# A third buffer for x projections, a group norm whose second part is written two projections later, and three 1/rms chains instead of five

## The chip, the cores and the metric

The kernel runs on one core of one Trainium2 chip. Its time is the device time in microseconds of one execution. Three executions of the kernel before took 2889.99 us in the median (2886.86 to 2891.28). The change is judged by the same time of the changed kernel.

## The reference

One inference step of a decoder trunk with two layers, on 16 meta tokens plus 1024 prompt tokens and on 8 sampled sequences of 8 tokens (1104 rows of 1024 features). Layer 0 is a Mamba-2 mixer and a SwiGLU feed-forward; layer 1 is sliding-window attention and a SwiGLU feed-forward. The change touches the mixer alone:

```
u   = rmsnorm(h) ; z, xBC, dt = split(u @ w_in)        # 1/rms of each row
x,B,C = silu(conv4(xBC) + b)                            # causal conv of width 4
y   = SSD(x * dt, a, B, C) + D * x                      # chunks of 128, 4 groups
v   = y * silu(z)
v   = v * rsqrt(mean over a group's 512 features of v*v + eps) * gain
h   = h + v @ w_out
```

Each of the four groups has 512 x features (four tiles of 128), 128 B and 128 C features, 512 z features and its own norm.

## The kernel before, in words

Each fp32 matrix product is done as three matmuls on split operands (L73 to L75: high by high, high by low, low by high). Features lie on partitions and rows (tokens) on the free dimension. The mixer goes over the rows in two halves: the first has 592 columns (80 sampled and meta rows, then 512 prompt rows; five blocks), the second 512 (four blocks). A projection is one 128-wide column tile of `w_in` against all rows of the half: 48 matmuls of 296 columns in the first half, 24 of 512 in the second. Its weights are loaded, split by ScalarE (L150) and by VectorE or GpSimd (L156), and kept in DRAM for the second half.

In each half four groups follow one another. Beside the SSD of group g (`ssd`, `chunk_in`, `chunk_out`, and in the first half `decode`, which carries the eight sampled states through TensorE) the function `fill_pieces` writes the dense work, one projection at a time: four z projections with the gate of group g-1 (`gate`), the norm of group g-1, the projections of group g+1 (`xbc`: B, C, then four x tiles, each followed by its conv on ScalarE and VectorE), and the output projection of older groups (`out`, which adds into the residual, L832). Beside the last group, g = 3, there is no g+1, and z of group 3 is projected ahead into a tile of the x tag (`gate_ahead`).

`norm` is a generator in two parts. The first sums the squares by a matmul with ones (L803), scales (L804) and computes 1/rms by ten small VectorE instructions (`rsqrt`, L89 to L98). The second spreads the factors over partitions: for each block VectorE makes a diagonal matrix (L811), TensorE multiplies it with ones into an accumulator of the projections' own ring (L812; two accumulators in the first half, three in the second); then VectorE scales each x tile (L816), ScalarE and VectorE split it (L79, L80) into yH and yL for `out`. The tag xT, which holds the four x tiles of a group or z of group 3, has two buffers, so that x of group g+1 reuses the buffer of group g-1, which is free when the norm of g-1 has read it.

The order on each engine is written by a planner that works with its own model of the durations, with the order of the program as priority; the SSD is written with a priority 300 ahead of the dense work. Each engine then goes through its queue in that fixed order.

At the start `input_half` goes over the blocks: square with a row sum on ScalarE (L370), scale (L372), the `rsqrt` chain, transposes of the raw rows (L382), the scaled rows (L387), their transposes (L392) and the split. In the second half blocks go in pairs through one chain, in the first each block has its own. At the end of the mixer `out` of the last group in the second half saves each finished residual tile to DRAM (`FeedForward.save`, L1261), with the DMA issued from SP.

Of the kernel before, what the change touches and what calls it, by code (L numbers as in the profile page):

```python
# [10 lines left out]
F32 = mybir.dt.float32  # L11
# [66 lines left out]
def split_copy(nc, H, L, src):  # L78
    nc.scalar.copy(H, src)  # L79
    nc.vector.tensor_tensor(L, src, H.bitcast(F32), ALU.subtract)  # L80
# [130 lines left out]
def load_params(K, I):  # L211

    nc = K.nc
    buf = K.scratch
    row = 0
    for nm, n in GAINS:
        src = I["ffn_norm_g"][int(nm[3])] if nm.startswith("ffn") else (I[nm] if nm in ("kv_norm_g", "final_norm_g") else I[nm][0])
        nc.sync.dma_start(buf[row : row + n, 3072:3200], src.rearrange("(k p) -> k p", p=128))
        row += n
    for i, nm in enumerate(("ssm_dt_bias", "ssm_A_log", "ssm_D")):  # L220
        nc.sync.dma_start(buf[:, 3200 + 32 * i : 3232 + 32 * i], I[nm][0].partition_broadcast(128))
    nc.sync.dma_start(buf[:4, :3072], I["ssm_conv_w"][0])
    nc.sync.dma_start(buf[4:5, :3072], I["ssm_conv_b"])
    nc.sync.dma_start(buf[32:56, :3072], I["state_conv"][0].rearrange("b k c -> (b k) c"))
# [44 lines left out]
class Mamba:  # L269
# [59 lines left out]
    def input_half(self, hf):  # L329
        nc, K = self.nc, self.K  # L330
        self.u = []
        for nm in ("uH", "uL"):
            for i in range(2):
                self.u.append(self.up.tile([128, 4, 592], F32R, name=f"{nm}{i}", tag=f"{nm}{i}"))
        H2, L2 = self.u[:2], self.u[2:]
        self.uH = [H2[k // 4][:, k % 4, :] for k in range(KD)]
        self.uL = [L2[k // 4][:, k % 4, :] for k in range(KD)]
        blocks = HALVES[hf]["blocks"]
        rows = {}

        def load(c):
            if c < len(blocks):
                rows[c] = self.load_rows(hf, c)

        if hf == 0:
            v = self.small([128, 2], "xv")
            nc.gpsimd.memset(v[:], 0.0)
            nc.scalar.activation(v[:, 0:1], v[:, 1:2], AF.Square)
        for c in range(2):
            load(c)  # L350
        gb = [self.tmp("gb") for _ in range(2)]
        for i in range(2):
            nc.sync.dma_start(gb[i][:, :512], self.I["ssm_norm_g"][0, 512 * i : 512 * i + 512].partition_broadcast(128))
        if hf == 0:
            for c in range(2, 5):
                load(c)
            load_params(K, self.I)
            self.wdt = self.kp.tile([128, KD, 32], F32, name="wdt")
            nc.sync.dma_start(self.wdt[:], self.I["ssm_w_in"][0, :, 5120:5152].rearrange("(k p) m -> p k m", p=128))
        self.rtok = []  # L360
        groups = ((0,), (1,), (2,), (3,), (4,)) if hf == 0 else ((0, 1), (2, 3))
        for cs in groups:
            nr = blocks[cs[0]][1]
            v = self.small([128, 2], "xv")
            xns = [self.quad("xn") for _ in cs]
            if hf == 1 and cs[0] == 0:
                for c in range(2, 4):
                    load(c)
            for i, c in enumerate(cs):
                nc.scalar.activation(xns[i][:nr], rows[c][:nr], AF.Square, accum_out=v[:nr, i : i + 1])  # L370
            w = v[:nr, : len(cs)]
            nc.vector.tensor_scalar(w, w, 1.0 / D, EPS, ALU.mult, ALU.add)  # L372
            r = rsqrt(nc, self.wk, w, len(cs), f"rx{cs[0]}")
            self.rtok += [r[:, i : i + 1] for i in range(len(cs))]
            for i, c in enumerate(cs):
                o, n = blocks[c]
                xr, xn = rows[c], xns[i]
                for kh in range(2):
                    ps = self.ps()
                    for j in range(4):  # L380
                        k = 4 * kh + j
                        nc.tensor.transpose(ps[:, 128 * j : 128 * j + n], xr[:n, 128 * k : 128 * k + 128], K.ident[:n, :n])  # L382
                    eng = nc.scalar.copy if kh else nc.vector.tensor_copy
                    eng(K.h[hf][:, 4 * kh : 4 * kh + 4, o : o + n], ps[:].rearrange("p (k c) -> p k c", k=4)[:, :, :n])
                for kh in range(2):
                    ks = slice(512 * kh, 512 * kh + 512)
                    nc.vector.scalar_tensor_tensor(xn[:n, ks], xr[:n, ks], r[:n, i : i + 1], gb[kh][:n, :512], ALU.mult, ALU.mult)  # L387
                for kh in range(2):
                    ps = self.ps()
                    for j in range(4):  # L390
                        k = 4 * kh + j
                        nc.tensor.transpose(ps[:, 128 * j : 128 * j + n], xn[:n, 128 * k : 128 * k + 128], K.ident[:n, :n])  # L392
                    pv = ps[:].rearrange("p (k c) -> p k c", k=4)[:, :, :n]
                    split_copy(nc, H2[kh][:, :, o : o + n], L2[kh][:, :, o : o + n], pv)
                yield
            if hf == 0 and 1 in cs:
                self.W.load()
# [140 lines left out]
    def xbc(self, hf, g, which):  # L538
        G = self.Gs[g]
        if 0 in which:  # L540
            G.BC = [None] * 2
        for i in which:
            wH, wL = self.W.get()
            acc = self.project(self.H, wH, wL, self.uH, self.uL)
            if i < 2:
                out = G.BC[i] = self.gp.tile([128, 592], F32, name="bcT", tag="bcT", bufs=4)
                ci = 16 + 4 * i + g
            else:
                if i == 2:
                    G.xt = self.gp.tile([128, 4, 592], F32, name="xT", tag="xT", bufs=2)  # L550
                    G.x = [G.xt[:, t, :] for t in range(4)]
                out = G.x[i - 2]
                ci = 4 * g + i - 2
            self.conv(hf, acc, ci, out)
            yield
# [225 lines left out]
            yield  # L781

    def gate_ahead(self, G):
        z = self.gp.tile([128, 4, 592], F32, name="zT", tag="xT", bufs=2)
        G.z = [z[:, t, :] for t in range(4)]
        for t in range(4):
            self.gate_tile(lambda: G.z[t])
            yield
# [102 lines left out]
    def fill_pieces(self, hf, g):  # L891
        Gs = self.Gs
        yield from self.gate(g - 1)
        nrm = self.norm(Gs[g - 1], g - 1)
        next(nrm)
        if g < 3:
            yield from self.xbc(hf, g + 1, range(2))
        if g > 1:
            yield from self.out(Gs[g - 2], hf, which=range(2, 4))
        next(nrm)  # L900
        if g < 3:
            yield from self.xbc(hf, g + 1, range(2, 6))
            yield from self.out(Gs[g - 1], hf, which=range(2))
        else:
            yield from self.gate_ahead(Gs[3])
        if hf == 1:
            yield from self.state_out(g - 1)

# [295 lines left out]
class FeedForward:  # L1204
# [50 lines left out]
    def save(self, e, m=None):  # L1255

        h = self.K.h

        def to(e, a, src):
            fs = slice(0, KD) if m is None else slice(m, m + 1)  # L1260
            self.nc.sync.dma_start(self.saved[e][:, fs, a : a + src.shape[2]], src[:, fs])  # L1261

        if self.layer == 0:
            if e == 0:
                to(0, 0, h[0][:, :, 40:592])
                to(1, 0, h[0][:, :, 0:40])
            else:
                to(1, 40, h[1])
        else:
            to(e, 0, h[e][:, :, 8:552])  # L1270
# [1206 lines left out]
```

## Time and profile before

| | |
|---|---|
| median of three runs | 2889.99 us |
| the profiled execution's own time | 2894.77 us |
| its span, first to last instruction | 2893.0 us |
| TensorE busy | 2779.4 us, 96% |
| TensorE's weight loads busy | 2554.9 us, 88% |
| VectorE, ScalarE, GpSimd busy | 70%, 42%, 17% |
| mean granted TensorE clock | 0.981 |

The span is counted from the first instruction to the last; the execution's own time holds 1.8 us beside it. A granted clock of 1.00 is 2.4 GHz and 0.50 is 1.2 GHz; a mean in between tells how much of a stretch was spent at the lower of the two. The mixer fills roughly the first 1010 us. In the rows, "x" is a count of instructions, square brackets hold the idle time of the engine ahead of an instruction and what ended it, and "L812" is a line of the kernel before.

### The profile page before, as it was taken

What the parts mean: (1) busy time and instruction counts of PE and PEld (TensorE: products, weight loads), DVE (VectorE), ACT (ScalarE), POOL (GpSimd) and SP (SyncE); (2) the same over time, 40 slices, a digit from 0 to 9 for tenths busy, and PEclk for the clock granted to TensorE, in tenths of its full rate; (3) what the DMA queues carried; (4) which work ended last, traced back from release to release, by engine and by line L of the source; (5) the groups of instructions that cost most, each with busy time, mean ns of one, the idle gap of its engine ahead of it and who ended that gap; (6) DMA issues with size and microseconds to landing.
All of it is one profiled execution on the core that took longest, in us unless ns stands there. A gap on an engine that the chain in (4) does not pass through costs nothing.

```text
span 2893.0 us, 51252 instructions
## 1 busy us (share of the span) xinstructions
PE 2779.4 (96%) x19990; PEld 2554.9 (88%) x19990; DVE 2028.3 (70%) x3655; ACT 1221.7 (42%) x2580; POOL 488.4 (17%) x692
## 2 busy tenths in 40 slices
PE   7999999999999999999999999998999999999998
PEld 6877988887787799999999997666898999999998
DVE  6778676646665688777768792454569877877787
ACT  4666464337442344333342233455434433433224
POOL 1455453324223100000000002333210000000000
PEclk9999999999999999999999999999999999999999
DMA  6775856566554524434458662001533444437664
GB/s 200 233 230 188 273 191 219 182 226 220 166 191 149 186 75 154 161 138 134 149 205 328 238 215 94 19 22 45 172 104 98 168 136 145 159 137 300 236 222 155
DMA packets 327010, 496.58 MB, mean 172 GB/s; under 512 B 24480, under 2 KB 222560, under 8 KB 325714
## 3 DMA queue, kind: packets, MB, share of 16 engines
q1 hardware_dynamic: 326766, 493.30, 50.3%
q8 instruction: 158, 2.59, 0.4%
q14 instruction: 86, 0.70, 0.1%
HBM read 317.93 MB, written 175.30 MB: 170 GB/s over the span
## 4 chain that ended last, share of the span: by engine, by line
PE 83%; DVE 7%; DMA 4%; ACT 3%; issue 2%; POOL 1%; SPq 0%; ACTq 0%; DVEq 0%; POOLq 0%
PE wacc L1486 10%; PE wacc L1484 10%; PE wacc L1485 10%; PE acc L73 6%; PE acc L74 6%; PE acc L75 6%; PE dacc L1484 5%; PE dacc L1485 5%; PE dacc L1486 5%; PE pP L73 2%; PE pP L74 2%; PE pP L75 2%; PE ps L670 1%; PE ps L667 1%; DVE cc L585 1%
## 5 line engine op out<-in xcount | busy, mean ns | idle before, releaser
L1143 ACT CAST wo<-ws 128x512 fp32r<-128x512 f32 x428 | 263.7, 620 | 545.0 <-PE wacc L1485 241.8
L1484 PE MATMUL dacc<-bo,wo 128*128 128x276 f32 (+1 forms) x1232 | 359.9, 292 | 10.8 <-DMA bo<-f_B 7.0
L1485 PE MATMUL dacc<-bo,wo 128*128 128x276 f32 (+1 forms) x1232 | 357.3, 290 | 0.0
L1486 PE MATMUL dacc<-bo,wo 128*128 128x276 f32 (+1 forms) x1232 | 357.0, 290 | 0.0
L1144 DVE TENSOR_TENSOR wo<-ws,wo 128x512 fp32r<-128x512 f32 x428 | 297.8, 699 | 67.9 <-ACT wo L1143 58.9
L73 PE MATMUL acc<-uH,wH 128*128 128x296 f32 (+1 forms) x840 | 279.9, 333 | 0.9 <-DVE th L762 0.6
L74 PE MATMUL acc<-uL,wH 128*128 128x296 f32 (+1 forms) x840 | 278.6, 332 | 0.0
L75 PE MATMUL acc<-uH,wL 128*128 128x296 f32 (+1 forms) x840 | 276.8, 329 | 0.9 <-DVE wL L156 0.9
L1484 PEld LDWEIGHTS dacc<-bo,wo 128*128 128x128 f32 x1232 | 233.8, 190 | 12.7 <-issue 10.3
L1485 PEld LDWEIGHTS dacc<-bo,wo 128*128 128x128 f32 x1232 | 233.9, 190 | 0.0
L1486 PEld LDWEIGHTS dacc<-bo,wo 128*128 128x128 f32 x1232 | 233.6, 190 | 0.0
L73 PEld LDWEIGHTS acc<-uH,wH 128*128 128x128 f32 x840 | 161.9, 193 | 16.4 <-issue 4.1
L74 PEld LDWEIGHTS acc<-uL,wH 128*128 128x128 f32 x840 | 161.6, 192 | 12.7 <-issue 4.2
L75 PEld LDWEIGHTS acc<-uH,wL 128*128 128x128 f32 x840 | 161.4, 192 | 11.6 <-issue 2.0
L585 DVE SCALAR_TENSOR_TENSOR cc<-raw,convw,cc 128x616 f32<-128x616 f32 (+1 forms) x144 | 136.8, 952 | 41.0 <-ACT cc L583 39.1
L1632 DVE TENSOR_TENSOR hN<-hN,dacc 128x544 f32<-128x544 f32 (+1 forms) x164 | 116.1, 719 | 30.5 <-PE dacc L1486 26.0
L73 PE MATMUL acc<-yH,wH 128*128 128x296 f32 (+1 forms) x360 | 123.1, 343 | 10.9 <-ACT yH L79 5.1
L2278 POOL MEMSET mask<- 128x64 f32 x1 | 0.2, 154 | 723.8 <-PE dacc L1486 723.8
L74 PE MATMUL acc<-yL,wH 128*128 128x296 f32 (+1 forms) x360 | 120.9, 336 | 0.0
L75 PE MATMUL acc<-yH,wL 128*128 128x296 f32 (+1 forms) x360 | 120.4, 336 | 0.0
L1484 PE MATMUL wacc<-T2H,wo 128*128 128x276 f32 (+1 forms) x352 | 103.2, 295 | 4.2 <-ACT T2H L79 4.2
L1143 ACT CAST wo<-sum 128x512 fp32r<-128x512 f32 x66 | 41.0, 621 | 154.3 <-PE wacc L1485 110.9
(594 smaller groups left out, 8629.8 us busy)
## 6 DMA issues: line engine op xcount, KB each, us to landing
kept<-wH SPq DMA_DIRECT2D x56, 512.0 KB
kept<-wL SPq DMA_DIRECT2D x56, 512.0 KB
ws<-ffn_w_gate SPq DMA_DIRECT2D x44, 512.0 KB
ws<-ffn_w_up SPq DMA_DIRECT2D x44, 512.0 KB
ws<-ffn_w_down SPq DMA_DIRECT2D x44, 512.0 KB
ws<-ssm_w_in SPq DMA_DIRECT2D x40, 512.0 KB
wH<-kept SPq DMA_DIRECT2D x38, 512.0 KB
wL<-kept SPq DMA_DIRECT2D x38, 512.0 KB
```

The source lines that it names most:

```text
L73: nc.tensor.matmul(out, wH, xH, start=start, stop=False)
L74: nc.tensor.matmul(out, wH, xL, start=False, stop=False)
L75: nc.tensor.matmul(out, wL, xH, start=False, stop=stop)
L585: nc.vector.scalar_tensor_tensor(o, raw[:, k : k + n], w(k), o, ALU.mult, ALU.add)
L667: nc.tensor.matmul(pyv[64 * q : 64 * q + 64, t, :], xd[:n, t, q, :], Ev[:, 4 * q + t, :], start=True, stop=True)
L670: nc.tensor.matmul(pst[:], bt[lo:n], xw[lo:n].rearrange("p t q d -> p (t q d)"), start=True, stop=True)
L1143: nc.scalar.copy(H, src)
L1144: (low or nc.vector).tensor_tensor(L, src, H.bitcast(F32), ALU.subtract)
L1484: nc.tensor.matmul(out, wH, xH, start=start, stop=False, skip_group_check=True)
L1485: nc.tensor.matmul(out, wH, xL, start=False, stop=False, skip_group_check=True)
L1486: nc.tensor.matmul(out, wL, xH, start=False, stop=stop, skip_group_check=True)
L1632: add = lambda d, s: nc.vector.tensor_tensor(d, d, s, ALU.add)
```

## The change

Four edits. The tag xT gets three buffers. In `fill_pieces` the second part of the norm is written two projections later (after the first two x projections of g+1, or after two of the four tiles of `gate_ahead`). The first half's blocks share the 1/rms chain in pairs: block 0 alone, then 1 and 2, then 3 and 4. The eight saves of single tiles in layer 0 are issued from ScalarE's queue instead of SP's.

```diff
-        groups = ((0,), (1,), (2,), (3,), (4,)) if hf == 0 else ((0, 1), (2, 3))
+        groups = ((0,), (1, 2), (3, 4)) if hf == 0 else ((0, 1), (2, 3))
...
-                    G.xt = self.gp.tile([128, 4, 592], F32, name="xT", tag="xT", bufs=2)
+                    G.xt = self.gp.tile([128, 4, 592], F32, name="xT", tag="xT", bufs=3)
...
-        z = self.gp.tile([128, 4, 592], F32, name="zT", tag="xT", bufs=2)
+        z = self.gp.tile([128, 4, 592], F32, name="zT", tag="xT", bufs=3)
...
-        next(nrm)
+
         if g < 3:
-            yield from self.xbc(hf, g + 1, range(2, 6))
+            yield from self.xbc(hf, g + 1, range(2, 4))
+            next(nrm)
+            yield from self.xbc(hf, g + 1, range(4, 6))
             yield from self.out(Gs[g - 1], hf, which=range(2))
         else:
-            yield from self.gate_ahead(Gs[3])
+            ahead = self.gate_ahead(Gs[3])
+            for _ in range(2):
+                yield next(ahead)
+            next(nrm)
+            yield from ahead
...
     def save(self, e, m=None):
         h = self.K.h
+        start = (self.nc.sync if self.layer or m is None else self.nc.scalar).dma_start
         def to(e, a, src):
             fs = slice(0, KD) if m is None else slice(m, m + 1)
-            self.nc.sync.dma_start(self.saved[e][:, fs, a : a + src.shape[2]], src[:, fs])
+            start(self.saved[e][:, fs, a : a + src.shape[2]], src[:, fs])
```

## Rows read from the trace of the kernel before

**Rows 1.** The profile's page, head and busy times of the engines.

```profile
PE 2779.4 (96%) x19990; PEld 2554.9 (88%) x19990; DVE 2028.3 (70%) x3655; ACT 1221.7 (42%) x2580; POOL 488.4 (17%) x692
```

**Rows 2.** Who waited for whom, TensorE, 100 to 960 us: total, times, longest.

```profile
PE acc L812 <- DVE dg L811: 7.6, 3, 4.4
PE ps L630 <- DVE xT L589: 4.3, 2, 3.1
PE ps L720 <- DMA big<-state_ssm: 4.0, 2, 2.8
...
PE ps L667 <- DVE cb L633: 2.2, 1, 2.2
```

**Rows 3.** Busy time by stretch: length, engines' busy (instructions), TensorE clock, DMA.

```profile
211.00:229.00 18.00, 12.97 (x80) 9.68 (x79) 13.79 (x29) 6.58 (x15) 7.61 (x11) 0.62 0.84 270
469.00:488.00 19.00, 16.04 (x97) 12.78 (x96) 11.81 (x28) 8.87 (x26) 7.87 (x8) 0.73 0.52 166
732.00:744.00 12.00, 6.91 (x26) 5.43 (x25) 6.74 (x21) 8.79 (x21) 3.36 (x6) 0.72 0.45 151
926.00:933.00 7.00, 4.54 (x23) 3.58 (x21) 2.93 (x15) 0.59 (x1) 0.82 (x1) 1.00 0.12 37
```

**Rows 4.** The same view, instructions on the accumulators alone (acc: projections, L812).

```profile
437.00:451.00 14.00, 14.00 (x103) 13.81 (x103) 1.53 (x2) 1.31 (x2) 1.00 0.86 305
886.00:903.00 17.00, 16.63 (x72) 13.50 (x73) 1.38 (x2) 1.18 (x2) 1.00 0.55 201
211.00:229.00 18.00, 4.51 (x20) 4.58 (x20) 0.00 (x0) 0.73 (x2) 0.62 0.84 270
469.00:488.00 19.00, 8.99 (x37) 7.97 (x37) 0.00 (x0) 0.00 (x0) 0.73 0.52 166
```

**Rows 5.** TensorE in order of time: start, length, instruction, idle before it.

```profile
220.81 1.94 PE L720 MATMUL ps<-cmask_sb,big 128*128 128x128 f32 x8 [2.80 <-DMA big<-state_ssm]
475.44 0.77 PE L667 MATMUL ps<-big,xd 80*64 80x80 f32 x16 [2.16 <-DVE cb L633]
738.92 0.80 PE L812 MATMUL acc<-dg,cmask_sb 128*128 128x128 f32 x2 [4.36 <-DVE dg L811]
983.58 1.22 PE L73 MATMUL acc<-yH,wH 128*128 128x512 f32 x2 [3.43 <-ACT yH L79]
```

**Rows 6.** VectorE in order of time: first and last of two ten-step 1/rms chains.

```profile
214.43 0.28 DVE L89 TENSOR_SCALAR rs_i<-gv 128x5 int32<-128x5 int32 x1
222.15 0.16 DVE L98 SCALAR_TENSOR_TENSOR rg_y<-rs_t,rg_y 128x5 f32<-128x5 f32 x1
976.43 0.17 DVE L89 TENSOR_SCALAR rs_i<-gv 128x4 int32<-128x4 int32 x1
978.02 0.16 DVE L98 SCALAR_TENSOR_TENSOR rg_y<-rs_t,rg_y 128x4 f32<-128x4 f32 x1
```

**Rows 7.** VectorE and TensorE: last splits of a norm, first output projection after it.

```profile
756.99 1.33 DVE L80 TENSOR_TENSOR yL<-xT,yH 128x512 fp32r<-128x512 f32 x1
766.56 0.40 PE L73 MATMUL acc<-yH,wH 128*128 128x512 f32 x1
838.62 0.61 PE L812 MATMUL acc<-dg,cmask_sb 128*128 128x128 f32 x4
850.36 1.28 DVE L80 TENSOR_TENSOR yL<-xT,yH 128x512 fp32r<-128x512 f32 x2
863.85 0.40 PE L73 MATMUL acc<-yH,wH 128*128 128x512 f32 x1
```

**Rows 8.** The start, ScalarE, VectorE and TensorE in order of time.

```profile
20.69 1.06 ACT L370 ACTIVATE xn<-S 128x1024 f32<-128x1024 f32 x1 [2.21 <-issue]
25.91 1.23 DVE L156 TENSOR_TENSOR wL<-ws,wH 128x1024 fp32r<-128x1024 f32 x1 [1.66 <-ACT wH L150]
31.98 0.16 DVE L98 SCALAR_TENSOR_TENSOR rx_y<-rs_t,rx_y 128x1 f32<-128x1 f32 x1
41.54 0.41 PE L73 MATMUL acc<-uH,wH 128*128 128x296 f32 x1
```

**Rows 9.** The saves on SP, the load after them, ScalarE meanwhile.

```profile
996.42 16.85 SPq L1261 DMA_DIRECT2D res<-big  x8
1053.33 0.38 SPq L1164 DMA_DIRECT2D ws<-ffn_w_gate  x1
1004.75 0.63 ACT L1054 ACTIVATE sqh<-big 128x512 f32<-128x512 f32 x1 [3.25 <-DVE big L832]
```

## The prediction

> **What bounds the kernel now.** I read the page first: TensorE is busy 96% of the span [rows 1], so a gain has to come from its idle time or its clock. Next the list of who waited for whom on TensorE, cut to the mixer without its start and its end. There the longest entry is the one that the change touches: the factors' matmul L812 waits for VectorE's diagonal matrices L811, 7.6 us in three waits [rows 2]. The third view, busy time by stretch, is laid around each of the six places where the norm's second part begins beside an SSD. Four of them have idle time [rows 3]; at the other two (second group of each half), where output projections stand between the norm's two parts, TensorE doesn't stop.
>
> The four stretches are A (first half, g = 1), C (first half, g = 3), D (second half, g = 1) and F (second half, g = 3). The reader is to see two losses in each row: idle time, which is the length less TensorE's busy time, and clock, whose mean lies between 1.00 (2.4 GHz) and 0.50 (1.2 GHz). I price the clock as (1 - clock) x length x TensorE's busy share, since a slow clock costs nothing while TensorE idles.
>
> - A: idle 18.0 - 12.97 = 5.0; clock 0.38 x 18.0 x 0.72 = 4.9; together 10.0.
> - C: idle 19.0 - 16.04 = 3.0; clock 0.27 x 19.0 x 0.84 = 4.3; together 7.3.
> - D: idle 12.0 - 6.91 = 5.1; clock 0.28 x 12.0 x 0.58 = 1.9; together 7.0.
> - F: idle 7.0 - 4.54 = 2.5; clock 1.00, nothing; together 2.5.
>
> That is 26.7 us, 15.5 of idle time and 11.2 of clock.
>
> Why it stops there is seen in the same view for accumulator matmuls alone [rows 4]. In full flow 103 of them fit in 14 us (a first-half projection of 48 takes 6.5 us), and 72 second-half ones in 17 us (a projection of 24 takes 5.7 us). In A there are 20 in 18 us, in C 37 in 19 us. The projections written behind the norm's second part don't come before its first L812, and all that TensorE has meanwhile is the chain of the SSD and of decode: in A it stops at a load of the state, in C at cb, in D at L812 itself [rows 5]. What L812 waits for is the chain of ten small instructions: 7.9 us from first to last in A, 1.8 us where nothing is between them [rows 6].
>
> **The change part by part.** The sum is made against the profiled execution, 2894.8 us, which is 4.8 us above the median of the runs; at the end 4.8 us are taken off.
>
> *Norm's second part two projections later, and the third buffer that allows it.* No instruction is added or removed: four or five pairs of L811 and L812 and four each of L816, L79 and L80 per norm move behind two projections, with no DMA among them. The buffer itself costs no instruction. They are moved past two projections' weight splits on ScalarE and VectorE or GpSimd, two convs, and on SP past the loads and keeps of those weights. Between the norm's parts there are now 2 x 6.5 = 13.0 us of projections more in the first half, 11.3 us in the second; both cover the longest chain, 7.9 us. So in D and F, where the named wait is L812 itself, I count the whole loss: -(7.0 + 2.5) = -9.5 us. In A and C TensorE stands at decode's own waits. The two projections can fill these, if the planner puts them there; the waits for the state and for cb stay possible. Bounds: 0 and -17.3 us. I take half, -8.6 us, because 13.0 us of new work is more than the 5.0 and 3.0 us of idle time, but TensorE goes through its queue in order and a wait ahead of the filler would still stand.
>
> *What is late next.* The output projection of the same group now follows the second part by two projections instead of four, except beside g = 3, where it comes after the late gates. In the second half the second part takes from the first L812 to the last yL 758.3 - 738.9 = 19.4 us for g = 1 and 851.6 - 838.6 = 13.0 us for g = 2, and the output starts 27.6 and 25.2 us after the first L812 [rows 5, 7]. Four projections are 22.7 us of these; the rest, 4.9 and 2.5 us, is SSD work. With two projections and half the SSD work the cover is 13.8 and 12.6 us, short by 5.6 and 0.4 us. The first matmul of `out` would wait, and behind it everything in TensorE's queue. But the 19.4 us hold projection matmuls placed between the L812s, which come closer together where less is left to place. I take half of both, +3.0 us. Bounds: 0, and 19.4 us of latency against bare projections in all four fills: 2 x 8.1 + 2 x 6.4 = +29 us.
>
> *Three chains for the first half.* Two chains of ten instructions and their scaling go, 22 small VectorE instructions. What counts is when block 4 is through: its square ends at 21.9 us, but its own chain only at 32.0, behind block 3's and the first weights' split, which ends at 27.1 [rows 8]. A shared chain can be through before that split, so the last block can come 32.0 - 27.1 = 4.9 us earlier, and with it the first long run of projections, now at 41.5. Against it: block 3 has to wait for block 4's square, and at the stretched length of 7.9 us the shared chain ends at 29.8, 2.7 us after the split. Bounds -4.9 and +2.7; I take -2.4, half of the gain, since other transposes and copies lie between.
>
> *Saves from ScalarE.* SP's eight saves span 16.9 us, and the next load leaves SP at 1053.3, 40 us later [rows 9], so a freer SP brings nothing here. ScalarE gets eight issues; at SP's 0.38 us for one that is 3.0 us, in a stretch where it idles 3.25 us before one instruction. Bounds 0 and +3.0; I take 0, since each save waits for the same add as the square beside it and ScalarE has room.
>
> Sum: -9.5 - 8.6 + 3.0 - 2.4 + 0 = -17.5 us; 2894.8 - 17.5 = 2877.3; less 4.8, 2872 us.
>
> On the clock the trace says: after the waits of A, C and D the granted clock fell to its lower level, and the fall is 11.2 of the 26.7 us [rows 3]. The Trainium skill ("TensorE: Matmul & The Clock Gate", Part 1) has it that the cost of ramping up is under 1% of a typical span and not worth fitting. By that rule the clock terms would be dropped: D and F give 7.6, A and C half of 8.0, and the sum would be 7.6 + 4.0 + 2.4 - 3.0 = 11.0, so 2879 us. I keep the clock: in this kernel the losses at stake are themselves under 1%.
>
> **The rivals.**
>
> *The named waits alone.* A and C keep their loss, because decode's load and cb hold TensorE, not the norm. For it: A's longest idle time is ended by a DMA [rows 5]. Against it: so few projection matmuls in both stretches [rows 4]. -9.5 - 2.4 + 3.0 = -8.9: 2881 us.
>
> *The whole fill loosens.* A and C go entirely, `out` doesn't wait, and the two waits of the transposes L630 for the last x tile's conv (4.3 us [rows 2]), at the change of groups, go with an order that has slack. -26.7 - 2.4 - 4.3 = -33.4: 2857 us. Against it: the convs of the last two x tiles now share VectorE with the norm's scaling and splits.
>
> *The output waits for the norm (slower).* In all four fills with an `out` the second part takes its 19.4 us. Cover: 13.8 us in the second half, 13.0 + 2.5 = 15.5 in the first. So 2 x 5.6 + 2 x 3.9 = 19.0 us of waits, and a clock that falls after them as in D (1.9 for 5.1 idle) adds 7.1: +26.1. With the gain of A and C lost it ends at 26.1 - 9.5 - 2.4 = +14.2: 2904 us. The one such wait that the trace shows, where a norm is followed at once by its output, was 3.43 us [rows 5]. It decides from the point where the second part takes longer than 14 to 15.5 us; with 13.0 us, as for g = 2, it doesn't arise.
>
> *Nothing moves.* The planner orders by its own model; if it places the same projections as before, the third buffer goes unused: 2890 us.
>
> **How the numbers follow.** Forecast 0.52, named waits alone 0.13, the fill loosens 0.12, output waits 0.15, nothing moves 0.08. Leaving out a tenth at each end gives 2856 to 2893; the forecast's own range is 2862 to 2884. About 0.2%, 5.8 us, is what a measurement can tell from no change. Faster by more: 0.52 + 0.12 and most of the named waits (0.10), 0.74. Within: the rest of these, most of nothing moves and a mild wait, 0.12. Slower: 0.14.
>
> **What would show it.** Right: projection matmuls in the places of A and C at the rate of full flow; L812's waits under 1 us; no half clock there; the chain of the last two blocks over before 29 us. Wrong: waits of `out`'s first matmul for yH or yL of over 3 us in the fills; TensorE still stopped at decode's load with few accumulator matmuls; longer waits of L630. The prediction fails if the idle time of TensorE between 100 and 960 us doesn't fall by about 10 us.

## The result, and the profile after

The changed kernel takes 2870.73 us (median of six runs, 2866.08 to 2873.31), the kernel before 2890.71 us (six runs beside them, 2886.86 to 2895.34): a ratio of 0.9938, 95% interval [0.9926, 0.9951], so 0.6% faster. The forecast was 2872 us. The profiled execution of after took 2869.85 us, 24.9 us less than that of before; the medians differ by 20.0 us, because the profiled execution of before was 4.1 us above its median and that of after 0.9 us below. What follows accounts for the 24.9.

The lines of after that answer to [rows 1, 2]: the page's busy times, then TensorE's waits from 100 to 960 us (total, times, longest).

```profile
PE 2760.2 (96%) x19990; PEld 2545.5 (89%) x19990; DVE 2022.5 (71%) x3633; ACT 1222.4 (43%) x2580; POOL 487.1 (17%) x692
```

```profile
PE ps L392 <- DVE xn L387: 5.5, 1, 5.5
PE acc L812 <- DVE dg L811: 4.4, 5, 2.4
PE acc L73 <- ACT yH L79: 3.7, 2, 2.1
PE ps L630 <- DVE xT L589: 2.7, 2, 2.3
```

TensorE has the same 19990 matmuls and is busy 19.2 us less: a matmul at half clock counts as busy, so part of the loss was never in the idle time. In the list the load of `big<-state_ssm` and `cb` [rows 2] are gone, L812 is down from 7.6 to 4.4 us, and a new wait, for `xn`, stands first.

Busy time by stretch (length; PE, PEld, DVE, ACT, POOL busy; TensorE clock; DMA share, GB/s), to be held against [rows 3]: the norm's second part in A, C, D and F, where it stands in after, in stretches as long as those of before. Then two places that [rows 3] don't have: B, beside the third SSD of the first half, and the start of the second half.

```profile
225.00:243.00 18.00, 18.00 (x145) 15.88 (x144) 17.67 (x30) 13.98 (x39) 9.31 (x15) 1.00 0.98 331
470.00:489.00 19.00, 19.00 (x154) 17.58 (x154) 17.27 (x29) 14.59 (x34) 14.21 (x16) 1.00 0.71 236
723.00:735.00 12.00, 12.00 (x62) 10.06 (x61) 9.65 (x16) 6.96 (x11) 3.75 (x7) 1.00 0.52 188
908.00:915.00 7.00, 7.00 (x36) 5.79 (x35) 2.86 (x9) 1.71 (x3) 1.28 (x1) 1.00 0.59 185
366.00:384.00 18.00, 14.80 (x102) 13.60 (x102) 16.29 (x23) 8.67 (x17) 4.43 (x8) 0.91 0.48 169
507.00:519.00 12.00, 6.23 (x38) 5.78 (x37) 9.81 (x20) 5.40 (x9) 4.39 (x4) 0.72 0.20 61
```

In the first four TensorE doesn't stop and the clock is 1.00; in before they had 15.5 us of idle time and clocks of 0.62, 0.73, 0.72 and 1.00. The accumulators alone (same columns without POOL), A and C, against [rows 4]:

```profile
225.00:243.00 18.00, 12.49 (x82) 10.92 (x81) 3.14 (x4) 0.71 (x2) 1.00 0.98 331
470.00:489.00 19.00, 13.57 (x87) 12.19 (x88) 3.81 (x5) 0.66 (x1) 1.00 0.71 236
```

82 and 87 accumulator matmuls where there were 20 and 37: projections now fill these stretches.

Where the time went can be followed by TensorE alone. Both kernels have 19990 matmuls; the start of the n-th in after, less that in before, is how far after is ahead. Worked out from the two traces, by the time of before:

```
stretch of before (us)            after gains (-) or loses (+)
0-60    the start                  -1.5
60-205                             -1.3
205-310 A                         -10.8
310-365                            +0.1
365-385 B                          +5.5
385-410 change of groups           -5.9
410-465                            -1.4
465-530 C                          -9.7
530-600 second half's start        +6.0
600-725                            +0.2
725-850 D                          -6.4
850-920                            -0.1
920-970 F                          -6.0
970-1060 end of the mixer          +4.4
1060-end                           +1.9     in all -24.8 (rounding)
```

The order of instructions differs, so within a stretch the n-th matmul isn't the same work in both; only sums over stretches mean something. F's 6.0 is more than the 3.2 us of idle time that before has there, and I read it together with the mixer's end: -1.6. The profiled execution of before also took longer than most of its kernel. That of e3 below, a kernel with the same time as before by the medians, is 7.5 us ahead of it in the same count, 2.7 of them in A. So of A's 10.8 us some 8 belong to the change (an estimate from one execution of each).

The new losses, in TensorE's order of time (start, length, instruction, idle before it): L812 in B, the start of the second half, and the first matmul after the mixer; the first line answers to A's in [rows 5].

```profile
218.85 0.63 PE L720 MATMUL ps<-cmask_sb,big 128*128 128x128 f32 x4 [1.01 <-DVE rs_i L89]
...
369.55 0.49 PE L812 MATMUL acc<-dg,cmask_sb 128*128 128x128 f32 x2 [2.43 <-DVE dg L811]
370.81 0.80 PE L812 MATMUL acc<-dg,cmask_sb 128*128 128x128 f32 x2 [0.77 <-DVE dg L811]
...
513.03 1.94 PE L392 MATMUL ps<-cmask_sb,xn 128*128 128x128 f32 x8 [5.52 <-DVE xn L387]
...
983.85 0.37 PE L1491 MATMUL wacc<-B11H,wo 128*128 128x276 f32 x1 [2.62 <-ACT sqh L1060]
```

What VectorE does meanwhile, in after: ahead of B's L812 three conv taps and three diagonal matrices; at the second half's start the 1/rms chain of the first two row blocks, from its first step to its last, with gate products in between.

```profile
365.64 2.65 DVE L585 SCALAR_TENSOR_TENSOR cc<-raw,convw,cc 128x616 f32<-128x616 f32 x3 [1.65 <-ACT cc L583]
368.21 2.71 DVE L811 TENSOR_SCALAR dg<-cmask_sb,rg_y 128x128 f32<-128x128 f32 x3
...
503.64 0.15 DVE L89 TENSOR_SCALAR rs_i<-xv 128x2 int32<-128x2 int32 x1
503.71 2.82 DVE L768 TENSOR_TENSOR xT<-xT,zT 128x592 f32<-128x592 f32 x4
506.45 1.41 DVE L90 TENSOR_SCALAR rs_i<-rs_i 128x2 int32<-128x2 int32 x1
...
510.74 0.16 DVE L98 SCALAR_TENSOR_TENSOR rx_y<-rs_t,rx_y 128x2 f32<-128x2 f32 x1
```

SP's queue suggests why nothing else could run then: the buffers of `ws` hold row blocks (`xr`), and the load of the output projection's next weights is issued only when the rows have been read. e8 tests this.

```profile
480.59 0.42 SPq L326 DMA_DIRECT2D xr<-x_prompt  x1
...
493.80 0.42 SPq L326 DMA_DIRECT2D xr<-x_prompt  x1
...
513.68 0.38 SPq L114 DMA_DIRECT2D ws<-ssm_w_out  x1
```

### The profile page after: what moved, and what is told of

Its sections match the earlier page's. It is cut to its first block, busy times and chain, and to the rows that moved or that the text cites. A ratio compares the mean times of both kernels' runs of the same rounds, so it can differ in the third digit from the quotient of the medians.

```text
span 2868.1 us, 51222 instructions
## 1 busy us (share of the span) xinstructions
PE 2760.2 (96%) x19990; PEld 2545.5 (89%) x19990; DVE 2022.5 (71%) x3633; ACT 1222.4 (43%) x2580; POOL 487.1 (17%) x692
## 5 line engine op out<-in xcount | busy, mean ns | idle before, releaser
L73 PE MATMUL acc<-uH,wH 128*128 128x296 f32 (+1 forms) x840 | 276.5, 329 | 1.7 <-DVE th L762 1.6
L74 PE MATMUL acc<-uL,wH 128*128 128x296 f32 (+1 forms) x840 | 275.5, 328 | 0.0
L73 PEld LDWEIGHTS acc<-uH,wH 128*128 128x128 f32 x840 | 158.9, 189 | 16.7 <-issue 6.6
L74 PEld LDWEIGHTS acc<-uL,wH 128*128 128x128 f32 x840 | 158.8, 189 | 10.6 <-issue 2.2
L73 PE MATMUL acc<-yH,wH 128*128 128x296 f32 (+1 forms) x360 | 122.3, 342 | 6.9 <-ACT yH L79 3.7
L74 PE MATMUL acc<-yL,wH 128*128 128x296 f32 (+1 forms) x360 | 120.6, 336 | 0.1
L1491 PE MATMUL wacc<-N4H,wo 128*128 128x276 f32 (+1 forms) x352 | 102.7, 292 | 4.7 <-DVE hN L1504 2.4
```

The source lines that it names most:

```text
L73: nc.tensor.matmul(out, wH, xH, start=start, stop=False)
L74: nc.tensor.matmul(out, wH, xL, start=False, stop=False)
L1491: nc.tensor.matmul(out, wH, xH, start=start, stop=False, skip_group_check=True)
```

## The experiments

Theory: the norm's later second part carries the gain, by giving TensorE projections ahead of its first L812. Rivals: the chains, the buffer alone, or SP's relief carry it. Later ones ask how late is best, what holds the projections back, and what the new losses are. "Lead" is the count of the table above, against the kernel before.

**e1_norm_only**: after, with five chains and with the saves on SP.

```diff
-        groups = ((0,), (1, 2), (3, 4)) if hf == 0 else ((0, 1), (2, 3))
+        groups = ((0,), (1,), (2,), (3,), (4,)) if hf == 0 else ((0, 1), (2, 3))
...
-        start = (self.nc.sync if self.layer or m is None else self.nc.scalar).dma_start
+        start = self.nc.sync.dma_start
```

> The third buffer and the norm's second part two projections later, without the shared chains and with the saves on SP. Theory filler (two projections fill TensorE between the norm's two parts): the four stretches A, C, D, F lose their 26.7 us, fresh waits cost about 5, so 20 to 22 us under the kernel before, about 2869 us, the same as the changed kernel. Rival parts (chains and saves carry a third or more of the gain): at most 13 us under the kernel before, 2877 us or more.

2870.32 us, ratio 0.9939 [0.9926, 0.9953]: all of the gain. By stretches: A -9.6, B +6.0, change of groups -5.9, C -9.7, second half's start +6.3, D -6.4, F -6.0, as in after. Its start gains 2.8 us without shared chains.

**e2_saves_on_sp**: after, with the second of these two edits alone.

> The changed kernel with the saves back on SP. In the changed kernel's trace the lead over the kernel before falls from 31.4 to 27.1 us where the mixer ends. Theory saves cost (ScalarE's issues are behind that): 3 to 4 us under the changed kernel, about 2867 us. Rival saves free (the fall has another cause there): within 2 us of the changed kernel, 2870 us.

2871.09 us, 0.9941 [0.9926, 0.9955]. The end of the mixer (970 to 1060 us of before) loses 4.3 us here too: within these intervals the saves from ScalarE neither cost nor bring.

**e3_buffer_only**: before, with three buffers.

```diff
-                    G.xt = self.gp.tile([128, 4, 592], F32, name="xT", tag="xT", bufs=2)
+                    G.xt = self.gp.tile([128, 4, 592], F32, name="xT", tag="xT", bufs=3)
...
-        z = self.gp.tile([128, 4, 592], F32, name="zT", tag="xT", bufs=2)
+        z = self.gp.tile([128, 4, 592], F32, name="zT", tag="xT", bufs=3)
```

> The kernel before with the third buffer of the x tag and nothing else. Theory filler: the order of the program holds the projections back, not the buffer, so no gain, within 4 us of the kernel before, 2890 us, and the waits of the factors' matmul L812 stay. Rival buffer (the two buffers hold back the x projections of the next group): 10 us or more under the kernel before, 2880 us or less.

2887.90 us, 0.9999 [0.9989, 1.0010]: nothing. TensorE's waits, 100 to 960 us, are much as in before [rows 2]:

```profile
PE acc L812 <- DVE dg L811: 7.2, 3, 4.2
PE ps L630 <- DVE xT L589: 5.7, 3, 3.3
PE ps L720 <- DMA big<-state_ssm: 2.3, 2, 2.1
...
PE ps L667 <- DVE cb L633: 2.2, 1, 2.2
```

**e4_chains_only**: before, with three chains in the first half (the `groups` line of after alone).

> The kernel before with the three shared 1/rms chains and nothing else. Theory: the first long run of projections starts 1.5 us earlier, as in the changed kernel's trace, 2888 to 2890 us. Rival (the planner's new order of the start moves later waits too): over 4 us away from the kernel before, either way, with the stretches A or C changed.

2897.61 us (twelve runs, 2886.04 to 2907.95), 1.0031 [1.0017, 1.0044]: 9.5 us slower, which the theory excluded and the rival allowed (over 4 us either way, with A changed). In its trace the start is 0.5 us later than in before and A loses 6.0 us; it has these two waits:

```profile
220.50 1.94 PE L720 MATMUL ps<-cmask_sb,big 128*128 128x128 f32 x8 [4.56 <-DMA big<-state_ssm]
...
285.51 0.44 PE L630 MATMUL ps<-cmask_sb,xT 128*80 128x128 f32 x1 [3.07 <-DVE xT L589]
```

The first was 2.80 us in before [rows 5] and 2.11 us in e3. The profiled execution of before, 2894.77 us, lies so far above the medians of its kernel that the excess hardly shows against it; that of e3, 2887.01 us, is close to them. Against e3's e4's profiled execution is 9.4 us longer, and by the count of matmuls 8.7 us of that are lost in A. Most of them come behind the first wait, where TensorE runs part of the time at half clock in e4, but not in e3 (225 to 245 us, e4 first):

```profile
225.00:245.00 20.00, 20.00 (x120) 16.87 (x119) 13.91 (x25) 12.79 (x37) 4.57 (x8) 0.88 0.49 147
```

```profile
225.00:245.00 20.00, 20.00 (x168) 18.18 (x167) 16.38 (x29) 14.89 (x41) 8.11 (x10) 1.00 0.69 203
```

So the chains alone gain nothing, and the excess lies in A. Why A runs worse with shared chains stays open, and so does the scatter of 22 us.

**e5_one_later**: after, the second part one projection later instead of two.

```diff
-            yield from self.xbc(hf, g + 1, range(2, 4))
+            yield from self.xbc(hf, g + 1, range(2, 3))
             next(nrm)
-            yield from self.xbc(hf, g + 1, range(4, 6))
+            yield from self.xbc(hf, g + 1, range(3, 6))
...
-            for _ in range(2):
+            for _ in range(1):
```

> The changed kernel with the norm's second part one projection later instead of two (one x projection, or one tile of gate_ahead, between). Theory filler: one projection is 6.5 us in the first half, less than the 7.9 us chain of A but more than its 5.0 us of idle time, so most of A and C and all of D and F go: 2870 to 2877 us. Rival (two projections are needed, since the clock falls at any rest of a wait): A and C stay half, 2879 us or more.

2880.16 us, 0.9969 [0.9957, 0.9980]: half of the gain. TensorE's waits, 100 to 960 us, and one of them, in A, with the VectorE instruction that holds up its chain:

```profile
PE acc L812 <- DVE dg L811: 9.2, 6, 3.0
```

```profile
221.28 2.92 DVE L156 TENSOR_TENSOR wL<-ws,wH 128x1024 fp32r<-128x1024 f32 x1
224.62 0.58 PE L812 MATMUL acc<-dg,cmask_sb 80*128 80x80 f32 x2 [2.38 <-DVE dg L811]
```

One projection, 6.5 us, isn't enough: L812 still stops, six times. In A a weight split of 2.92 us stands ahead of the last step of the chain. The time is the rival's, but its picture isn't: by the count of matmuls A and C gain 8.6 and 7.7 us, D 4.2 and F 1.8. Nor does the clock fall at any rest of a wait, as the rival has it: L812 waits 2.46 us in D and 3.04 us in F, and the granted clock is 1.00 from 720 to 745 and from 905 to 940 us. The profiled execution, 2874.29 us, is the fastest of six, so its trace shows less than the whole loss.

**e6_four_later**: after, the second part behind all four x projections or gate tiles, directly ahead of `out`.

```diff
-            yield from self.xbc(hf, g + 1, range(2, 4))
+            yield from self.xbc(hf, g + 1, range(2, 6))
             next(nrm)
-            yield from self.xbc(hf, g + 1, range(4, 6))
...
-            for _ in range(2):
+            for _ in range(4):
```

> The changed kernel with the norm's second part four projections later, directly ahead of the output projections that read it. Theory output waits (the second part takes 13 to 19 us and nothing else is left for TensorE): out's first matmul waits 5 us or more in each of four fills and the clock falls behind it, 2895 to 2915 us. Rival (the planner puts SSD work of the next group into the place): 2870 to 2880 us.

2909.46 us, 1.0074 [1.0061, 1.0086]: slower than before, as the theory had it. Its waits (100 to 960 us), and three places of `out` in the second half by stretch:

```profile
PE acc L812 <- DVE dg L811: 9.3, 7, 3.6
PE acc L74 <- DVE yL L80: 7.1, 6, 2.2
...
PE acc L73 <- DVE xT L816: 3.0, 2, 1.8
```

```profile
763.00:778.00 15.00, 8.58 (x32) 6.20 (x32) 11.68 (x19) 7.08 (x16) 3.39 (x4) 0.77 0.22 76
866.00:880.00 14.00, 9.92 (x45) 7.67 (x45) 11.89 (x33) 6.00 (x12) 0.19 (x1) 0.76 0.29 95
958.00:970.00 12.00, 7.81 (x29) 5.78 (x28) 8.50 (x12) 5.09 (x9) 4.18 (x4) 0.75 0.32 110
```

This is the mechanism of the rival "the output waits for the norm", at its place (L73 and L74 of `out`) and with its clock: real, but here with no projection left as cover. It takes effect in the second half: by the count of matmuls A and C still gain 4.2 and 5.5 us, while D loses 3.7, the 70 us behind it 6.6, and F gains nothing. At two projections no such wait is among those of the fills.

**e7_ring**: before, with the second half's factors (L812) in the SSD's ring instead of the projections' ring.

```diff
-        rb = self.acc()
+        rb = self.ps() if self.accw == 512 else self.acc()
```

> The kernel before, with the norm's factors of the second half (512 columns) in a tile of the SSD's PSUM ring instead of the projections' accumulator ring; the first half and the order of the program stay. Theory ring (the accumulator reserved for the factors is what holds the next projections behind the first L812): D and F lose their waits, 7.0 + 2.5 us, 2879 to 2882 us. Rival order (it is the program's order alone): D and F keep them, 2887 to 2891 us.

2890.95 us, 1.0014 [1.0004, 1.0024]. Its waits from 680 to 960 us, the new one in order of time, and the stretches of D and of that wait:

```profile
PE acc L73 <- DVE zT L762: 6.6, 1, 6.6
```

```profile
937.23 0.79 PE L73 MATMUL acc<-uH,ws 128*128 128x512 f32 x1 [6.57 <-DVE zT L762]
```

```profile
725.00:745.00 20.00, 20.00 (x108) 16.23 (x107) 11.85 (x30) 4.18 (x7) 3.63 (x10) 1.00 0.51 180
930.00:945.00 15.00, 8.43 (x31) 6.63 (x29) 8.81 (x14) 6.49 (x11) 2.57 (x2) 0.77 0.28 88
```

L812 no longer waits in the second half, D is full and gains 6.0 us, about as in after. So in the second half it was the place of L812 in the projections' ring that held them back; for the first half, with two accumulators, this wasn't tried. But with two buffers z of group 3 can't be written before the norm has read x of group 2. The first step of that z (L761) starts only behind the norm's last split:

```profile
935.86 1.57 ACT L761 ACTIVATE zT<-acc 128x512 f32<-128x512 f32 x3 [1.79 <-DVE yL L80]
```

TensorE waits 6.57 us for it, the mean clock there is 0.77, and F loses 4.0 us where after gains 6.0. That wait asks for the third buffer; the other ring together with three buffers wasn't run, and neither was the later second part with two.

**e8_rows_in_buffer**: after, with the second half's first two row blocks loaded into the idle third buffer of xT, which leaves both `ws` to weights.

```diff
+        elif hf == 1:
+            if c == 0:
+                t = self.gp.tile([128, 4, 592], F32, name="xrT", tag="xT", bufs=3)
+                self.xrows = t[:].rearrange("p t c -> p (t c)")
+            xr = self.xrows[:, 1024 * c : 1024 * c + 1024]
```

> The changed kernel, with the rows of the second half's first two blocks loaded into the idle third x buffer instead of the two weight buffers. In the changed kernel TensorE waits 5.5 us at 507.5 us for the scaled rows, and the clock is halved for 6.8 us behind it. Theory weights (the rows hold both weight buffers, so that no output projection is there to fill): the wait goes, 5 to 9 us under the changed kernel, 2862 to 2866 us. Rival chain (the 1/rms chain itself is late, and other work ahead of it in VectorE's queue): within 3 us of the changed kernel.

2868.75 us, 0.9932 [0.9920, 0.9945]: the fastest median of all, by 1.6 us, which these intervals don't tell from after. By its time the rival holds. The 5.52 us wait became 1.78 us at a matmul of `out`:

```profile
510.91 0.38 PE L73 MATMUL acc<-yH,wH 128*128 128x296 f32 x1 [1.78 <-DVE rs_t L91]
```

The second half's start now loses 3.5 us instead of 6.0: the weights explain part of it. The rest fits the VectorE chain behind the gates, of which the new wait names a step (L91); that wasn't tested by itself.

**e9_combined**: e8's edit on e1.

> The changed kernel with the second half's first two row blocks loaded into the idle third x buffer, and with five chains of 1/rms and SyncE's saves as before the change. Theory (the norm's later second part carries the whole gain, chains and saves are worth nothing, and what the rows' buffer saves is given back behind it): 2866 to 2871 us, a ratio to the kernel before of 0.993 to 0.994. Rival (the shared chains cost, as they did without the later norm, 7 to 9 us that the changed kernel's gain hides): 2860 to 2863 us.

2870.57 us, 0.9939 [0.9927, 0.9952]: no sum of gains, and no hidden cost of the chains. With chains shared the later norm gave ratios of 0.9938 (after), 0.9941 (e2) and 0.9932 (e8), without 0.9939 (e1) and 0.9939 (e9).

**e10_second_fill_early**: after, but with the old place of the second part beside the third SSD of each half.

```diff
+        if g == 2:
+            next(nrm)
         if g < 3:
             yield from self.xbc(hf, g + 1, range(2, 4))
-            next(nrm)
+            if g != 2:
+                next(nrm)
```

> The changed kernel, but beside the third SSD of each half (g = 2), where output projections stand between the norm's two parts, the second part begins where it did before the change. Theory (the new waits of 2.43 and 0.77 us and the half clock there were an exchange against the wait at the change of groups that they did away with): the lead over the kernel before is about 5 us larger behind g = 2 of the first half and falls back by 5 to 6 us at about 400 us, where L630 waits for the conv again by about 3 us; 2869 to 2873 us in all. Rival (the new waits are a loss of their own, and the boundary's gain comes from the third buffer): the lead stays, 2864 to 2867 us. Second rival (g = 2 of both halves gains by the later place too, in work that no wait shows): 2876 us or more.

2870.38 us, 0.9943 [0.9927, 0.9960]: the same. L812 no longer stops in B, and the wait at the change of groups is back, 3.39 us against 3.1 in before (0.4 in after):

```profile
389.07 0.31 PE L630 MATMUL ps<-cmask_sb,xT 128*80 128x128 f32 x1 [3.39 <-DVE xT L589]
```

By stretches B is 0.0 and the change of groups -0.7, against +5.5 and -5.9 in after: an exchange. I had put it wrongly in one point: against before, which has the same wait, the lead doesn't fall back at the change of groups, it merely isn't gained there; and ahead of it it was 3.4 us larger than after's, not 5, because A gave 2.3 us less.

## Why the prediction was right, point by point

**The place and the mechanism: right, shown by e1, e3 and e7.** The projections came into the four stretches, TensorE no longer stops there, the clock stays up. e1 has the whole gain without chains and saves, e3 none with the buffer alone, and e7 shows for the second half that the place of L812 held the projections back. Two of the signs named came in part only: A and C hold 82 and 87 accumulator matmuls, not the 132 and 140 of full flow (103 in 14 us [rows 4]), since the SSD runs between them; and L812 still waits 2.43 us, in B. Idle time between 100 us and the same point near 960 us of before, from the rows of before and of after, fell by 38.0 - 26.1 = 11.9 us, about the 10 asked for:

```profile
100.00:960.00 860.00, 822.02 (x5372) 712.76 (x5371) 565.64 (x934) 436.21 (x999) 329.79 (x394) 0.97 0.61 204
```

```profile
100.00:935.00 835.00, 808.95 (x5389) 705.83 (x5388) 559.57 (x936) 435.37 (x996) 328.65 (x394) 0.99 0.63 212
```

**A and C at half: the term that was mis-sized.** I took -8.6 of -17.3 us, for fear that decode's load and `cb` would hold TensorE ahead of the filler. They didn't: A gave 10.8 and C 9.7 us, 20.5 together, or 17.5 if e3's profiled execution is taken for before: about their whole. In A the wait for the state is gone, and the load has more time: in before it left at 216.60 us, 4.2 us ahead of that matmul (220.81 us [rows 5]), in after at 212.54, 6.3 us ahead of it (218.85 us); before first, then after:

```profile
216.60 0.37 SPq L714 DMA_DIRECT2D big<-state_ssm  x1
```

```profile
212.54 0.37 SPq L714 DMA_DIRECT2D big<-state_ssm  x1
```

**D and F whole.** D: -6.4 for -7.0. F: -6.0, with the mixer's end -1.6, for -2.5. Sound for D; for F the figure lies between the two.

**The clock counted as loss: right.** The trace: A and C together had 8.0 us of idle time and gave 20.5 us (17.5 against e3), and the granted clock there went from 0.62 and 0.73 to 1.00. Counted by idle time alone A and C would have been worth 8.0 us at most, and the measurement decides against that. The Trainium skill ("TensorE: Matmul & The Clock Gate", Part 1) puts the ramp penalty at under 1% of a typical kernel span. That agrees in size, since the whole change is 0.6%; but the page says it of a kernel's warm-up, and leaving out what the clock loses behind later waits was the prediction's own reading of it.

**What is late next: the wrong places.** I took +3.0 us for `out` waiting for yH and yL. In the fills there is none; the 3.7 us for yH in the table are both at the ends of the halves, behind group 3 (1.64 and 2.09 us), where before had such waits too: 1.64 us at 565.85 us and 3.43 us [rows 5]. Instead the start of the second half lost 6.0 us and B 5.5, of which the change of groups returned 5.9. The second half's start I hadn't looked at: a lead of 25 us brings TensorE to the rows while their chain still stands behind four gate products (2.82 us), and the projections of the first half that stood beside the rows in before have been used up by then (before was busy 14.2 of the 15 us from 520 to 535). Most of the 4.4 us that the end of the mixer lost isn't due to the later norm: every kernel that I ran loses 1.9 to 4.4 us there, and e3, e4 and e7, which keep the old norm, 2.6 to 3.2. Whether before has a better order at that place, or its one profiled execution was lucky there, wasn't found.

**Three chains -2.4: wrong.** The start gained 1.5 us, but kernels without shared chains gained 0.0 (e3), 2.2 (e9), 2.8 (e1) and 4.4 (e7), and e4 with them lost 0.5. The last blocks' chain was to be over before 29 us and its last step came at 30.20, 1.8 us earlier than in before [rows 8]: the split still stands between its first step and its last.

```profile
24.99 0.17 DVE L89 TENSOR_SCALAR rs_i<-xv 128x2 int32<-128x2 int32 x1
26.27 1.22 DVE L156 TENSOR_TENSOR wL<-ws,wH 128x1024 fp32r<-128x1024 f32 x1
30.20 0.16 DVE L98 SCALAR_TENSOR_TENSOR rx_y<-rs_t,rx_y 128x2 f32<-128x2 f32 x1
```

**Saves at 0: right** (e2).

So the mechanism was right, but that 2872 us was hit so closely is luck: the errors of the sum cancel. A and C gave 11.9 us more than counted (8.9 against e3); the second half's start took 6.0 where 3.0 were set aside elsewhere; and 5 us of the profiled difference aren't in the medians. Of the rivals, "named waits alone" is refuted by A and C, "nothing moves" by the table; "the fill loosens" (2857 us) was right in A and C and in the change of groups (L630 4.3 to 2.7 us), but without what is late next. "The output waits" is e6.

## What to carry to other kernels

Where an in-order engine runs dry, look for the instruction that reserves the filler's buffers in program order and waits for a long small chain; move it behind as much filler as the chain lasts, and check that a cover of the same length remains in front of its consumer: one projection was too little, four too many. Price such a stretch with its clock, not its idle time alone. And count on part of it being lost at the next place where the faster engine arrives early.

## What the runs showed of the hardware

Small VectorE instructions can stretch beside a GpSimd instruction. In after a diagonal matrix L811 takes 0.28 us at 231.21 us. Of the three at 368.21 us, 2.71 us together, the first two run beside this weight split on GpSimd and take 1.29 and 1.34 us; the third, when the split is over, takes 0.28 us again. They are what L812 in B waits for.

```profile
367.75 2.90 POOL L156 TENSOR_TENSOR wL<-ws,wH 128x512 fp32r<-128x512 f32 x2 [3.18 <-ACT wH L150]
```

Likewise a step of 1/rms on 2 columns takes 0.15 us at 503.64 us, but 1.41 us at 506.45 us (L90), beside a GpSimd product of 1.49 us (L775) that starts at 506.35 us. Moving that work to another engine wasn't tried.
